# One pool for values and joining gate, running products behind the next subtraction, and an uneven share of filler in a stick-breaking attention block

## The chip, the cores and the metric

The kernel runs on one core of one Trainium2 chip. The time is device microseconds of that core, from one launch; lower is better. The time before is the median of three runs.

## The reference

One decoder block on a sequence of 1024 tokens with 1024 channels and 16 heads of 64, float32 throughout. Two branches start from one normalized input, are gated, and are joined.

```python
def stick_breaking_attention(q, k, v):
    # A[t,s] = sigmoid(z_ts) * prod_{s<j<t} (1 - sigmoid(z_tj)), s < t
    ...
    z = jnp.einsum('bhqd,bhkd->bhqk', qb, kb).astype(jnp.float32) * SB_SCALE
    ...
    w = jnp.where(mask, jnp.exp(jax.nn.log_sigmoid(z) + suffix), 0.0)
    outs.append(jnp.einsum('bhqk,bhkd->bhqd', w.astype(vb.dtype), vb))

def hybrid_layer(x, c, ...):
    mod = jax.nn.silu(c) @ w_ada + b_ada
    shift, scale, gate = jnp.split(mod, 3, axis=-1)
    h = rms_norm(x, norm_gain) * (1.0 + scale[:, None, :]) + shift[:, None, :]
    q, k, v, z_a, u, z_b, m_a, m_b = jnp.split(h @ w_in, offs, axis=-1)
    attn = stick_breaking_attention(to_heads(q), to_heads(k), to_heads(v))
    p_a = (attn * jax.nn.silu(z_a)) @ w_branch_a
    pooled = multiscale_causal_pool(u, pool_w, pool_scale)
    p_b = (pooled * jax.nn.silu(z_b)) @ w_branch_b
    merged = jax.nn.sigmoid(m_a) * p_a + jax.nn.sigmoid(m_b) * p_b
    return x + gate[:, None, :] * (merged @ w_out)
# the output is rms_norm of this
```

## The kernel before

The sequence is held in reverse order, so that the product over the tokens between a key and its query becomes a running product from left to right. Every float32 operand of a large matmul is split in two parts, a high one (a cast by ScalarE, `act.copy`) and a low one (a subtraction, mostly by VectorE), and a product is three matmuls: high x high, high x low, low x high. So wherever a matmul has a new operand, a cast and a subtraction stand before it.

**Order of the work.** A planner places the instructions: it takes the program as traced, simulates it with costs of its own, and on each engine and each queue issues next the earliest traced instruction that is ready in its simulation. An instruction called through `order(...)`, while `pinned` is set, is fixed behind the instruction traced before it on its engine. All matmuls of the attention are pinned, and so are the products `be * om`. The subtractions of the turns, the casts and (before) the scans are not. A buffer's next user waits for the last reader of that buffer. A pool that closes gives its memory to later pools, whose tiles wait for those tiles that had lain in their place.

**Stages, in order of time.** Input norm and modulation; the pooling branch's projection `u`; the values (`seven("v", ...)`, tiles named `vp`); the joining gate m_b (`seven("m", ...)`, tiles `mp`); the gate z_b of the pooling branch (`wzb`); the product with `w_branch_b` (`bp`); the attention with the remaining projections between its parts; the product with `w_branch_a`, the join and the product with `w_out`.

**seven().** A 1024x1024x1024 product as seven products of 512x512x512 instead of eight (p1, p5, p6, p7, p4, p3, p2, in this order), each of 2 x 24 matmuls. Its weights come by SyncE's DMA queue (`raw(first, ...)`): the first operand of a sum into a buffer `raw` of the pool `wts`, which all stages share, the other one (`a22`, `a11s`, `a21d`) into a buffer `ar` of the pool that is handed in as `sums`. Both have two buffers. For p5, `a_s1` loads `a21`, `a22` and `a11s`, adds the first two (L576), and subtracts `a11s` (L578) into `s2k`, which p6 and p3 read again. Then `a_op` makes the cast (L548) and the low part (L549), and `b_op` the same for the other operand (`bhl`, L554, L555). The profile drops digits from names: `ma` is `a11`, `a12`, `a21` or `a22` of the gate, `ma11s` its `a11s`, `va` the values' loads. The values use the pool `vs`, stored through `vo` buffers by `values`. That pool is closed and the pool `ms` is opened for the gate, whose results go through `go` buffers.

**Attention.** Eight pairs of heads; in each pair eight units (p, h, t), a head h and a quarter t of the queries (two rows of 128 queries, widths W from 1024 down to 128), in the order `HT_ORDER`: t = 0, 2, 0, 2, 1, 3, 1, 3. One step of the loop belongs to each unit, so a pair has steps 0 to 7. A step holds:

- `av_items(unit)`: for each chunk of 256 keys (4, 2, 4, 2, 3, 1, 3, 1 chunks in steps 0 to 7) a *turn* and a product. A turn transposes the weights of the chunk two further on (`wt`, into one of two PSUM banks `tr`), casts them (L947), subtracts (L948) and calls `flush()`. At the end `finish` adds the halves of the result (`tp`, L974).
- `z_items` of the unit three further on (t = 2, 1, 3, 1, 3, 0, 2, 0 in steps 0 to 7): logits (`z`), two sigmoids (`om` = 1 - beta, L921, and `be` = beta, L922), a mask by GpSimd (L926), a scan over `om` (the running product, L928) and the product `be * om`. The product is not issued there: it is put on the list `behind` and issued by the next `flush()`.
- a number of *quanta* of the projections (`fill`), three 512 wide matmuls each (`p`). A pair gets 55 of them, shared by `SHARE`:

```python
upto = QUANTA[p] * sum(SHARE[:k + 1]) // sum(SHARE)
step(ahead.get(p * 8 + k, []), p * 8 + k, upto - used)
```

With the even `SHARE` this is 6, 7, 7, 7, 7, 7, 7, 7. Within a step the quanta are spread evenly between the items. The projections' own VectorE work is a subtraction or product per half tile of eight quanta (`klo`, `qlo`, `za`); GpSimd makes the low parts of their weights (`w`, L116).

Lines that the text speaks of: `flush` and `behind`, `z_items` (L902 to 931 of the kernel before), `turn` (L933), `finish` (L964), `step` (L1022).

Of the kernel before, what the change touches and what calls it, by code (L numbers as in the profile page):

```python
# [9 lines left out]
F32 = mybir.dt.float32  # L10
F32R = mybir.dt.float32r
# [4 lines left out]
P = 128  # L16
# [10 lines left out]
NBE = (4, 4)  # L27
SHARE = (7,) * 8
DEPTH = 2
# [22 lines left out]
def block_kernel(ctx, tc, a, out):  # L52
# [3 lines left out]
    def pool(name, **kw):  # L56
        return tc.tile_pool(name=name, bufs=1, reuse_waits="tile", **kw)
# [500 lines left out]
    def k2(t, q):  # L558
        return t[:, 2 * q:2 * q + 2]
# [5 lines left out]
    def seven(nm, sums, load, b_of, a_moves, ta, tb, final, direct):  # L565

        s2k = sums.tile([P, 4, 512], F32, name=nm + "s2k")

# [62 lines left out]

    with pool("vp") as vp:

# [33 lines left out]

        def h_parts(nm, pl):
            def of(name, q):
                if name in ("p1", "p2", "p3"):  # L670
                    k, n = dict(p1=(0, 0), p2=(1, 0), p3=(1, 1))[name]
                    return lambda m, e: hT[:, m, 4 * k + 2 * q + e, 512 * n:512 * n + 512]
                return b_op(k2(tq[("p5", "p6", "p7", "p4").index(name)], q), pl, 2, f"{nm}{name}b{q}")
            return of

        with pool("vs", side="right") as vs:

            def load_v_w(t, m, k, q):
                nc.sync.dma_start(t.rearrange("p k c -> p (k c)"), a["w_v"][m, 2 * k + q])

            def values(m, n, j, src):
                sb = 4 * n + j
                vo = vs.tile([P, 8, 2, HD], F32R, tag="vo", bufs=3, name=f"vo{sb}_{m}")
                pv = src.rearrange("p (h d) -> p h d", d=HD)
                act.copy(vo[:, :, 0], pv)
                v.tensor_sub(vo[:, :, 1], pv, vo[:, :, 0].bitcast(F32))
                nc.sync.dma_start(
                    v_d[4 * m:4 * m + 4, :, sb].rearrange("n p c -> p n c"),
                    vo.rearrange("p (n h) i d -> p n (h i d)", h=2).bitcast(F32),
                )  # L690

            seven("v", vs, load_v_w, h_parts("v", vs), True, ("av", "tr"), ("pj", "z"), values, True)

        with pool("ms", side="right") as ms:

            def load_m_w(t, m, k, q):
                nc.sync.dma_start(t.rearrange("p k c -> p (k c)"), a["w_mb"][m, 2 * k + q])

            def gate_b(m, n, j, src):
                t = ms.tile([P, 512], F32, tag="go", bufs=3, name=f"sb{4 * m + j}_{n}")  # L700
                act.activation(t, src, AF.Sigmoid)
                nc.sync.dma_start(sb_d[4 * m + j][:, 512 * n:512 * n + 512], t)

            seven("m", ms, load_m_w, h_parts("m", ms), False, ("pj", "z"), ("av", "tr"), gate_b, True)

# [68 lines left out]
    with pool("at") as at:  # L774
# [63 lines left out]
        def projections():  # L838
# [16 lines left out]
            for i, (ct, p, use) in enumerate(todo):  # L855
# [6 lines left out]
                if gate:  # L862
                    out_ = sigmoid_out(at, 3, use[p], f"m{ct}")
                for sh in range(2):
# [37 lines left out]
        def z_items(u):  # L902
# [4 lines left out]
            for qb in (2 * t, 2 * t + 1):  # L907
                n0 = qb * P
                W = S - n0
                om = atz.tile([P, S], F32, tag="om", bufs=2, name=f"om{p}_{h}_{qb}")  # L910
                g = t // 2
# [3 lines left out]
                for i in range(nch):  # L915
# [11 lines left out]
                    if i == nch - 1:  # L927
                        v.tensor_tensor_scan(om[:, :W], om[:, :W], om[:, :W], 1.0, ALU.mult, ALU.min)  # L928
                        behind.append(lambda be=be, om=om, W=W: order(v.tensor_mul)(be[:, 1:W], be[:, 1:W], om[:, :W - 1]))
                        rows.append(be)  # L930
# [33 lines left out]
        def finish(u):  # L964
# [4 lines left out]
            if h == 0:  # L969
                both[t] = at.tile([P, 256], F32, tag="tp", bufs=3, name=f"tp{p}_{t}")  # L970
            tp = both[t]
# [236 lines left out]
```

## Time and profile before

| | |
|---|---|
| time, median of 3 runs | 1203.88 us (1203.19 to 1203.93) |
| the profiled execution: its time / its span | 1206.08 us / 1204.3 us |
| TensorE busy | 1174.5 us, 98% of the span |
| VectorE busy | 861.4 us, 72% |
| ScalarE busy | 563.9 us, 47% |
| GpSimd busy | 241.6 us, 20% |
| granted TensorE clock, mean | 0.996 |
| scans `om` (L928) | 128, 183.6 us |
| products `be` | 128, 101.1 us |
| subtractions `wt` (L948) | 160, 99.0 us |

How to read the profile: an engine is busy while an instruction runs on it. Matmuls are pipelined and their ends are modelled, so a busy TensorE isn't necessarily at its peak. A row of the groups has the line, the engine, the operation, output and inputs, shapes and count, then busy time, the mean length of one in ns, the idle time before these instructions and what ended it. A row in order of time has start, length in us, engine and operation, and in brackets the idle time before it and what ended that. A row of a stretch has its bounds and length, and then for each engine its busy time and number of instructions, the granted clock, the busy share of the DMA engines and GB/s.

### The profile page before, as it was taken

Reading aid. Unit: us, or ns where it says so; the run is one execution under the profiler, and the core shown is the slowest. Engines: PE = TensorE matmul, PEld = TensorE weight load, DVE = VectorE, ACT = ScalarE, POOL = GpSimd, SP = SyncE. Lnnn points to the kernel's source line nnn. Section 1 sums busy time; section 2 is a strip of 40 time slices with the busy share of each in tenths; the row PEclk is TensorE's granted clock in tenths of the full one; section 3 lists DMA queues with packets and bytes.
Section 4 is the critical chain, followed back from the end, with each engine's and each line's share of the span. In section 5 each row is a group of like instructions: output and inputs, shape, how many; then the busy total and the mean of one; then the engine's idle time right before and its main releaser. Section 6 shows DMA issues by size and latency. Waiting matters only on the chain.

```text
span 1204.3 us, 15853 instructions
## 1 busy us (share of the span) xinstructions
PE 1174.5 (98%) x5602; PEld 976.4 (81%) x5602; DVE 861.4 (72%) x1135; ACT 563.9 (47%) x1042; POOL 241.6 (20%) x376
## 2 busy tenths in 40 slices
PE   8999999899999999999999999999999999999997
PEld 7888888688888887887788878887878888888886
DVE  5767466554997651887888888879788885785643
ACT  5561363363223432656566566665656654232211
POOL 1000000000000003334343443435344441000001
PEclk9999999899999999999999999999999999999999
DMA  9652339546634357232323132422423115975612
GB/s 346 259 186 100 122 106 309 179 137 241 216 106 158 103 176 219 75 93 85 82 71 113 63 104 72 122 71 88 106 83 88 49 66 197 333 267 168 224 65 79
DMA packets 74753, 172.51 MB, mean 143 GB/s; under 512 B 9393, under 2 KB 22833, under 8 KB 72498
## 3 DMA queue, kind: packets, MB, share of 16 engines
q1 hardware_dynamic: 68770, 160.82, 40.9%
q10 hardware_dynamic: 5904, 10.68, 2.5%
q8 instruction: 44, 0.72, 0.2%
q14 instruction: 35, 0.29, 0.1%
HBM read 121.14 MB, written 33.56 MB: 128 GB/s over the span
## 4 chain that ended last, share of the span: by engine, by line
PE 81%; DVE 7%; issue 4%; DMA 4%; ACT 2%; POOL 1%; SPq 0%; POOLq 0%; ACTq 0%; DVEq 0%
PE p L101 21%; PE wzb L101 7%; PE pa L101 7%; PE bp L101 6%; PE o L101 6%; PE vp L101 6%; PE mp L101 5%; PE u L101 5%; PE z L101 4%; PE av L101 4%; PE wt L101 4%; DVE om L928 3%; PE ua L101 3%; PE wm L101 1%; DVE be L101 1%
## 5 line engine op out<-in xcount | busy, mean ns | idle before, releaser
L101 PE MATMUL p<-hT,w 128*128 128x512 f32 x1536 | 392.6, 392 | 0.0
L101 PEld LDWEIGHTS p<-hT,w 128*128 128x128 f32 x1536 | 283.0, 188 | 58.0 <-DVE klo L101 0.3
L928 DVE TENSOR_TENSOR_SCAN om<-om 128x512 f32<-128x512 f32 (+7 forms) x128 | 183.6, 1435 | 52.6 <-POOL om L926 27.4
L116 POOL TENSOR_TENSOR w<-w_raw,w 128x1024 fp32r<-128x1024 f32 x31 | 80.5, 2596 | 458.7 <-ACT w L121 453.6
L921 ACT ACTIVATE om<-z 128x512 f32<-128x512 f32 (+2 forms) x192 | 94.8, 493 | 130.6 <-PE z L101 99.3
L926 POOL TENSOR_SCALAR_AFFINE_SELECT om<-om 128x128 f32<-128x128 f32 x128 | 78.5, 613 | 182.2 <-ACT om L921 162.3
L948 DVE TENSOR_TENSOR wt<-wt,wt 128x512 fp32r<-128x512 f32 (+1 forms) x160 | 99.0, 620 | 20.8 <-ACT wt L947 20.3
L947 ACT CAST wt<-wt 128x512 fp32r<-128x512 f32 (+1 forms) x160 | 88.1, 551 | 46.8 <-PE wt L101 46.0
L101 PE MATMUL av<-wt,vv 128*128 128x512 f32 x320 | 106.0, 412 | 0.3 <-DVE wt L948 0.3
L101 PE MATMUL wt<-ident,be 128*128 128x128 f32 x576 | 90.8, 274 | 13.0 <-DVE wt L948 8.7
L101 DVE TENSOR_TENSOR be<-be,om 128x511 f32<-128x511 f32 (+7 forms) x128 | 101.1, 794 | 1.1
L922 ACT ACTIVATE be<-z 128x512 f32<-128x512 f32 (+2 forms) x192 | 94.1, 490 | 0.0
L101 PEld LDWEIGHTS wt<-ident,be 128*128 128x128 f32 x576 | 68.8, 140 | 30.1 <-DVE wt L948 9.3
L101 PE MATMUL pa<-ga,wa 128*128 128x512 f32 x384 | 89.6, 389 | 0.1
L101 PE MATMUL o<-wo,mhl 128*128 128x512 f32 (+1 forms) x408 | 89.6, 377 | 0.0
L101 PE MATMUL wzb<-hT,wzb 128*128 128x512 f32 x384 | 87.2, 389 | 0.0
L101 PEld LDWEIGHTS o<-wo,mhl 128*128 128x128 f32 x408 | 73.5, 188 | 14.1
L101 PEld LDWEIGHTS pa<-ga,wa 128*128 128x128 f32 x384 | 72.0, 188 | 15.4 <-DVE wa L116 0.5
L101 PEld LDWEIGHTS wzb<-hT,wzb 128*128 128x128 f32 x384 | 72.1, 188 | 15.0
L101 PE MATMUL z<-kl,q 128*128 128x512 f32 (+2 forms) x192 | 65.5, 341 | 0.0
L101 PE MATMUL z<-kh,q 128*128 128x512 f32 (+2 forms) x192 | 64.1, 334 | 1.3 <-DMA q<-qlo 1.3
L101 PE MATMUL u<-hT,wg 128*128 128x512 f32 x240 | 55.5, 391 | 0.0
(261 smaller groups left out, 1692.4 us busy)
## 6 DMA issues: line engine op xcount, KB each, us to landing
w_raw<-in_w_in SPq DMA_DIRECT2D x32, 512.0 KB, 3.5
v_d<-vo SPq DMA_DIRECT2D x16, 512.0 KB, 4.2
vv<-v_d SPq DMA_DIRECT2D x8, 1024.0 KB, 5.3
wa_raw<-in_w_branch_a SPq DMA_DIRECT2D x16, 512.0 KB, 4.6
wa<-in_w_mod SPq DMA_DIRECT2D x7, 1024.0 KB, 7.0
kh<-kh SPq DMA_DIRECT2D x48, 128.0 KB, 2.3
va<-in_w_v SPq DMA_DIRECT2D x10, 512.0 KB, 3.6
ma<-in_w_mb SPq DMA_DIRECT2D x10, 512.0 KB, 4.5
```

The source lines that it names most:

```text
L101: ins = op(*args, **kw)
L116: lo_eng.tensor_tensor(lo, src, hi.bitcast(F32), op=ALU.subtract)
L921: act.activation(om[:, b0:b0 + n], zp[:, :n], AF.Sigmoid, scale=-0.125)
L922: act.activation(be[:, b0:b0 + n], zp[:, :n], AF.Sigmoid, scale=0.125)
L926: gp.affine_select(out=tl[:, :P], in_=tl[:, :P], pattern=[[1, P]], compare_op=ALU.is_gt, fill=fill, base=0, channel_multiplier=-1)
L928: v.tensor_tensor_scan(om[:, :W], om[:, :W], om[:, :W], 1.0, ALU.mult, ALU.min)
L947: act.copy(wt[:, 0, :off], pt[:, :off])
L948: v.tensor_sub(wt[:, 1, :off], pt[:, :off], wt[:, 0, :off].bitcast(F32))
```

## The change

Four edits:

1. The pools `vs` and `ms` become one pool `vs`, which the values and the gate both use; it stays open until the gate is done, and closes together with the pool `vp`. The tile `s2k` gets one tag for all users, with one buffer.
2. The scan is no longer issued when its row's sigmoids are. It goes on the list `behind` together with its product, both pinned: so `flush()` issues them behind the subtraction of the next turn.
3. `SHARE` becomes 6, 8, 4, 8, 4, 9, 6, 10, which with 55 quanta a pair is also the number of quanta in steps 0 to 7.
4. `om` has three buffers instead of two; `sg` (sigmoid outputs of the other gate) and `tp` have two instead of three.

```diff
-SHARE = (7,) * 8
+SHARE = (6, 8, 4, 8, 4, 9, 6, 10)
...
-        s2k = sums.tile([P, 4, 512], F32, name=nm + "s2k")
+        s2k = sums.tile([P, 4, 512], F32, tag="s2k", bufs=1, name=nm + "s2k")
...
-    with pool("vp") as vp:
+    with ExitStack() as vps:
+
+        vp = vps.enter_context(pool("vp"))
...
+        vs = vps.enter_context(pool("vs", side="right"))
...
-        with pool("vs", side="right") as vs:
...
-            seven("v", vs, load_v_w, h_parts("v", vs), True, ("av", "tr"), ("pj", "z"), values, True)
-
-        with pool("ms", side="right") as ms:
...
-            def gate_b(m, n, j, src):
-                t = ms.tile([P, 512], F32, tag="go", bufs=3, name=f"sb{4 * m + j}_{n}")
...
-            seven("m", ms, load_m_w, h_parts("m", ms), False, ("pj", "z"), ("av", "tr"), gate_b, True)
...
+        def gate_b(m, n, j, src):
+            t = vs.tile([P, 512], F32, tag="go", bufs=3, name=f"sb{4 * m + j}_{n}")
...
+        seven("v", vs, loads("w_v"), h_parts("v"), True, ("av", "tr"), ("pj", "z"), values, True)
+        seven("m", vs, loads("w_mb"), h_parts("m"), False, ("pj", "z"), ("av", "tr"), gate_b, True)
...
-                    out_ = sigmoid_out(at, 3, use[p], f"m{ct}")
+                    out_ = sigmoid_out(at, 2, use[p], f"m{ct}")
...
-                om = atz.tile([P, S], F32, tag="om", bufs=2, name=f"om{p}_{h}_{qb}")
+                om = atz.tile([P, S], F32, tag="om", bufs=3, name=f"om{p}_{h}_{qb}")
...
-                        v.tensor_tensor_scan(om[:, :W], om[:, :W], om[:, :W], 1.0, ALU.mult, ALU.min)
-                        behind.append(lambda be=be, om=om, W=W: order(v.tensor_mul)(be[:, 1:W], be[:, 1:W], om[:, :W - 1]))
+
+                        def weights(be=be, om=om, W=W):
+                            order(v.tensor_tensor_scan)(om[:, :W], om[:, :W], om[:, :W], 1.0, ALU.mult, ALU.min)
+                            order(v.tensor_mul)(be[:, 1:W], be[:, 1:W], om[:, :W - 1])
+
+                        behind.append(weights)
...
-                both[t] = at.tile([P, 256], F32, tag="tp", bufs=3, name=f"tp{p}_{t}")
+                both[t] = at.tile([P, 256], F32, tag="tp", bufs=2, name=f"tp{p}_{t}")
```

More of the change, by code (lines that the diff above doesn't have):

```diff
@@ L666, in block_kernel, with h_parts @@
         early.close()
-        def h_parts(nm, pl):
+        vs = vps.enter_context(pool("vs", side="right"))
+        def h_parts(nm):
             def of(name, q):
@@ L672, in of @@
                     return lambda m, e: hT[:, m, 4 * k + 2 * q + e, 512 * n:512 * n + 512]
-                return b_op(k2(tq[("p5", "p6", "p7", "p4").index(name)], q), pl, 2, f"{nm}{name}b{q}")
+                return b_op(k2(tq[("p5", "p6", "p7", "p4").index(name)], q), vs, 2, f"{nm}{name}b{q}")
             return of
-        with pool("vs", side="right") as vs:
[L678 to L690, printed above, removed]
-            seven("v", vs, load_v_w, h_parts("v", vs), True, ("av", "tr"), ("pj", "z"), values, True)
@@ L694, in block_kernel, with loads, load @@
-        with pool("ms", side="right") as ms:
-            def load_m_w(t, m, k, q):
-                nc.sync.dma_start(t.rearrange("p k c -> p (k c)"), a["w_mb"][m, 2 * k + q])
-            def gate_b(m, n, j, src):
-                t = ms.tile([P, 512], F32, tag="go", bufs=3, name=f"sb{4 * m + j}_{n}")
-                act.activation(t, src, AF.Sigmoid)
-                nc.sync.dma_start(sb_d[4 * m + j][:, 512 * n:512 * n + 512], t)
-            seven("m", ms, load_m_w, h_parts("m", ms), False, ("pj", "z"), ("av", "tr"), gate_b, True)
+        def loads(w):
+            def load(t, m, k, q):
+                nc.sync.dma_start(t.rearrange("p k c -> p (k c)"), a[w][m, 2 * k + q])
+            return load
@@ new lines, in values @@
+        def values(m, n, j, src):
+            sb = 4 * n + j
+            vo = vs.tile([P, 8, 2, HD], F32R, tag="vo", bufs=3, name=f"vo{sb}_{m}")
+            pv = src.rearrange("p (h d) -> p h d", d=HD)
+            act.copy(vo[:, :, 0], pv)
+            v.tensor_sub(vo[:, :, 1], pv, vo[:, :, 0].bitcast(F32))
+            nc.sync.dma_start(
+                v_d[4 * m:4 * m + 4, :, sb].rearrange("n p c -> p n c"),
+                vo.rearrange("p (n h) i d -> p n (h i d)", h=2).bitcast(F32),
+            )
@@ L706, in block_kernel @@
+        def gate_b(m, n, j, src):
+            t = vs.tile([P, 512], F32, tag="go", bufs=3, name=f"sb{4 * m + j}_{n}")
+            act.activation(t, src, AF.Sigmoid)
+            nc.sync.dma_start(sb_d[4 * m + j][:, 512 * n:512 * n + 512], t)
+        seven("v", vs, loads("w_v"), h_parts("v"), True, ("av", "tr"), ("pj", "z"), values, True)
+        seven("m", vs, loads("w_mb"), h_parts("m"), False, ("pj", "z"), ("av", "tr"), gate_b, True)
     turns[0] = cycle(("av", "tr", "pj", "z"))
```

## The prediction

> **What bounds the kernel now.** I read the page first: busy times, then the forty slices.
>
> ```profile
> span 1204.3 us, 15853 instructions
> PE 1174.5 (98%) x5602; PEld 976.4 (81%) x5602; DVE 861.4 (72%) x1135; ACT 563.9 (47%) x1042; POOL 241.6 (20%) x376
> PE   8999999899999999999999999999999999999997
> DVE  5767466554997651887888888879788885785643
> PEclk9999999899999999999999999999999999999999
> ```
>
> TensorE is the bound: 1174.5 of 1204.3 us busy. None of its matmuls is removed, so the change can only take back idle time, 29.8 us in all, and time lost to a low clock. Two places stand out: the eighth slice, the only one with a lower granted clock, and the attention (slices 17 to 34), where VectorE is at 8 tenths.
>
> I then asked for stretches around the eighth slice and, for that place, the instructions in order of time.
>
> ```profile
> 215.00:240.00 25.00, 20.30 (x76) 15.88 (x75) 16.29 (x14) 8.22 (x10) 0.00 (x0) 0.86 0.44 151
> 240.00:265.00 25.00, 25.00 (x112) 20.70 (x111) 13.25 (x14) 16.16 (x22) 0.00 (x0) 1.00 0.38 124
> 220.00:225.00 5.00, 5.00 (x12) 3.94 (x13) 2.51 (x4) 1.04 (x1) 0.00 (x0) 0.50 0.90 313
> ...
> 147.95 1.23 DVE L583 TENSOR_TENSOR va11d<-va11d,va21d 128x1024 f32<-128x1024 f32 x1 [0.22 <-DMA va11d<-in_w_v]
> 205.01 11.04 PE L101 MATMUL mp<-hT,mp1a 128*128 128x512 f32 x48
> 209.55 1.28 SPq L697 DMA_DIRECT2D ma<-in_w_mb  x1
> 217.64 1.23 DVE L576 TENSOR_TENSOR ma<-ma,ma 128x1024 f32<-128x1024 f32 x1 [0.52 <-DMA ma<-in_w_mb]
> 218.90 1.04 ACT L548 CAST mp5a<-ma 128x1024 fp32r<-128x1024 f32 x1 [1.76 <-DVE ma L576]
> 220.00 13.95 PE L101 MATMUL mp<-mp5b,mp5a 128*128 128x512 f32 x48 [3.95 <-ACT mp5a L548]
> ```
>
> The columns after the length are PE, weight load, VectorE, ScalarE, GpSimd, granted clock, DMA share, GB/s. This is the gate's second product, p5. Its weight load `a22` is issued only at 209.55, the add that needs it starts at 217.64, the cast at 218.90, and TensorE stands still for 3.95 us. Then the clock is granted at 0.50 for the next 5 us (12 matmuls, no idle time shown). The stretch holds 76 matmuls where the next equal one holds 112: 36 matmuls at 25/112 = 0.223 us, so 8.0 us are lost here, idle and low clock together.
>
> For the attention I cut the time at the first matmul of each pair of heads (found by counting matmuls in program order) and asked what TensorE's transposes waited for.
>
> ```profile
> 502.30:566.28 63.98, 63.02 (x326) 52.96 (x325) 53.80 (x73) 40.19 (x87) 25.85 (x38) 1.00 0.27 77
> 566.28:632.72 66.44, 63.27 (x326) 52.82 (x325) 56.61 (x76) 39.96 (x86) 26.60 (x41) 1.00 0.32 87
> 891.89:957.79 65.90, 63.32 (x327) 52.87 (x325) 56.81 (x75) 39.73 (x86) 26.91 (x39) 1.00 0.30 85
> ...
> 549.62:558.99 9.37, 8.41 (x42) 6.61 (x41) 9.37 (x13) 4.05 (x9) 2.08 (x4) 1.00 0.01 2
> 617.41:625.43 8.02, 8.02 (x42) 6.69 (x41) 7.66 (x11) 5.09 (x10) 4.53 (x4) 1.00 0.00 1
> ...
> PE wt L101 <- DVE wt L948: 8.7, 9, 1.8
> PE wt L101 <- POOL tp L977: 2.2, 3, 1.1
> PE wt L101 <- DVE be L101: 1.9, 4, 0.6
> ```
>
> A pair without any wait: pair 0 took 63.98 us and had waits in one step alone, step 6, 9.37 us where the same step of pair 1 took 8.02; so 62.6 us. The first seven pairs run from 502.30 to 957.79, 455.5 us; seven quiet ones are 438.2. The prize here is 17.3 us. All of it is transposes waiting for VectorE: for the subtraction that frees their PSUM bank (both first rows; GpSimd is only named as the last releaser), or for a row of weights that isn't multiplied yet (`be`). VectorE is busy 53.8 to 56.8 us of a pair, so it has room on average and is late only in places:
>
> ```profile
> 686.52 1.67 DVE L101 TENSOR_TENSOR be<-be,om 128x895 f32<-128x895 f32 x2
> 687.74 0.30 PE L101 MATMUL wt<-ident,be 128*128 128x128 f32 x1 [0.59 <-DVE be L101]
> 697.61 2.40 POOL L116 TENSOR_TENSOR w<-w_raw,w 128x1024 fp32r<-128x1024 f32 x1 [1.75 <-ACT w L121]
> 697.69 0.60 PE L101 MATMUL wt<-ident,be 128*128 128x128 f32 x4
> 698.38 0.59 ACT L947 CAST wt<-wt 128x512 fp32r<-128x512 f32 x1
> 698.51 3.38 DVE L928 TENSOR_TENSOR_SCAN om<-om 128x896 f32<-128x896 f32 x1
> 702.37 0.69 DVE L948 TENSOR_TENSOR wt<-wt,wt 128x512 fp32r<-128x512 f32 x1
> 703.21 0.52 PE L101 MATMUL wt<-ident,be 128*128 128x128 f32 x3 [1.12 <-POOL tp L977]
> ```
>
> At 703.21 TensorE waits for the subtraction at 702.37, which stood behind a scan of 3.38 us; at 687.74 it waits for the product at 686.52.
>
> **The change, part by part.**
>
> *One pool.* The gate's `a22` and `a11s` loads go into the two `ar` buffers. In one pool these are free once the values' last reader of them is done, 147.95 + 1.23, instead of when the old pool's memory comes free; the two loads can be issued some 60 us earlier and also leave the crowded stretch around 210. Then the other operand, `a21`, waits only for the shared `raw` buffer as before, and the chain add 1.23, cast 1.04 starts when p1 is still running (until 216.05): it has to be 4 us earlier, and its late part is gone. I take 7.5 of the 8.0 us. Bounds: all 8.0; and 2.7, if `a21` or the second half now comes last and half the idle time and a third of the clock loss are saved (3.95/2 + 2.3/3; 2.3 is 22.4 - 12 matmuls at 0.223). The pool is larger by what only one side used (`vo` or `go`), so the later pools may wait for other buffers: the next stretches have no idle TensorE (240 to 265 above), and I cost that at nothing; if the cover failed it would be one wait for a load, up to 4 us like this one. `s2k` shared: its reader in the values ends with p3, before the gate's p5 writes it; nothing.
>
> *Scan behind the next subtraction.* No instruction is added or removed. The durations are those of the attention's groups (the last row is the page's, for GpSimd):
>
> ```profile
> L948 DVE TENSOR_TENSOR wt<-wt,wt 128x512 fp32r<-128x512 f32 x96 | 64.6, 673 | 11.4 <-ACT wt L947 11.1
> L974 DVE TENSOR_TENSOR tp<-av,tp 64x256 f32<-64x256 f32 x128 | 52.7, 413 | 2.6
> L928 DVE TENSOR_TENSOR_SCAN om<-om 128x896 f32<-128x896 f32 x15 | 33.5, 2231 | 0.4 <-ACT om L921 0.3
> L928 DVE TENSOR_TENSOR_SCAN om<-om 128x1024 f32<-128x1024 f32 x14 | 32.6, 2328 | 21.3 <-POOL om L926 12.0 <-ACT om L921 9.3
> L928 DVE TENSOR_TENSOR_SCAN om<-om 128x768 f32<-128x768 f32 x16 | 28.9, 1804 | 6.5 <-POOL be L926 3.4 <-ACT om L921 1.9 <-POOL om L926 1.1
> L928 DVE TENSOR_TENSOR_SCAN om<-om 128x640 f32<-128x640 f32 x16 | 27.7, 1730 | 5.1 <-ACT om L921 4.8 <-POOL be L926 0.3
> L928 DVE TENSOR_TENSOR_SCAN om<-om 128x512 f32<-128x512 f32 x15 | 18.5, 1235 | 1.7 <-POOL om L926 1.7
> L101 DVE TENSOR_TENSOR be<-be,om 128x1023 f32<-128x1023 f32 x14 | 18.1, 1291 | 0.0
> L101 DVE TENSOR_TENSOR be<-be,om 128x895 f32<-128x895 f32 x15 | 17.6, 1174 | 0.0
> L116 POOL TENSOR_TENSOR w<-w_raw,w 128x1024 fp32r<-128x1024 f32 x31 | 80.5, 2596 | 458.7 <-ACT w L121 453.6
> ```
>
> Before, a scan may start as soon as its sigmoids are there, so up to 2.3 us stand ahead of a subtraction. After, the subtraction goes first, and scan and product, 3.6 us for the longest row, stand behind it. The price: the rows get their weights later, and VectorE may idle where a scan is ready and its subtraction isn't. The tightest place is the row of 896 of the next pair, made at the end of step 5. Its scan now waits for step 6's first subtraction: transposes and cast (as from 697.69 to 698.97 above, 1.3 us), the subtraction 0.67, scan 2.23, product 1.17, together 5.4 us after the step begins, if VectorE is then free; wanted by the third turn of step 6, two thirds of 7.3 us plus its logits, about 5.2. So about 0.2 us of wait where VectorE is on time.
>
> *Shares.* A quantum is three matmuls, 0.67 us by the 0.223 above. VectorE's own work in a step is the scans and products of the two rows it makes, one subtraction a turn and two 0.41 us adds. Step 5 and step 7 (rows of 1024 and 896): 2.33 + 2.23 + 1.29 + 1.17 + 0.67 + 0.83 = 8.5 us. Steps 1 and 3 (768, 640; two turns): 1.80 + 1.73, about 0.95 + 0.8 for the products by their length, 1.3 + 0.83: 7.4. Steps 0 and 6 (512, 384), by length: about 7 and 6.3; steps 2 and 4 (256, 128): about 5.3 and 4.7. TensorE without waits, before: 8.3, 7.7, 8.7, 7.7, 7.6, 7.3, 8.0, 7.3 (sum 62.6). So steps 5 and 7 are over by 1.2 us each, which lands in the steps after them, 6 and 0: there lie the waits above (549.62 is a step 6, 697.69 a step 0). The quanta were 6 and then 7 a step; with 6, 8, 4, 8, 4, 9, 6, 10 TensorE's steps become 8.3, 8.4, 6.7, 8.4, 5.6, 8.6, 7.3, 9.3, each at or above VectorE's work.
>
> Following one pair through in these numbers leaves waits where turns come fastest: about 0.7 us in step 2 (its first subtraction behind scan and product of 640 and two adds), 0.3 in step 4, 0.2 in step 6; 1.2 us a pair against 17.3/7 = 2.5. That gives 7 x 1.3 = 9 us. The projections' six subtractions a pair (0.68 us each) and the scan blocked by GpSimd will fall badly in some pairs; I take 7. Bounds: all 17.3; and a loss of 5, if each pair's step 6 waits for the whole scan and product of 896 (3.4 us, less the 2.5 that go: 0.9 x 7 = 6, less a little at the others).
>
> *The rest, costed at nothing.* A third `om` buffer covers the rows' later release. `sg` and `tp` go from three buffers to two: the next user of a slot comes at least a whole step (5.6 us) after the store was issued. If that cover were gone, ScalarE would stand still for a store's landing. The query projection finishes four quanta closer to the step that uses it (7 quanta where 11 in the sixth pair, about 8.6 us, for a cast, a subtraction and one move); SP's queue order is otherwise unchanged.
>
> *A rule against the row at 698.51.* That scan of 896 took 3.38 us where its kind takes 2.23 on average; it began inside the 2.40 us GpSimd subtraction and ended 1.88 us after that one's end, so it looks as if it stood still until then: 1.15 us lost. The Trainium skill, "SBUF — State Buffer", section "Who interferes with whom", says that a VectorE instruction with two SBUF inputs and a GpSimd instruction that reads SBUF exclude each other, the later one waiting for the whole of the first; by that rule scan and product, now back to back, are one stretch of 3.4 us to be hit, and the 7 us of the attention would shrink towards nothing. This row agrees with it. From the rows alone: there are 31 such GpSimd subtractions in the kernel, some four a pair; two more hits a pair at 1.15 us would be 16 us of VectorE time, as much as the waits I expect to go. That is in rival (1).
>
> **Sum.** 7.5 + 7 = 14.5. The profiled execution took 1206.08 us (span 1204.3), the median of the runs 1203.88; I count from the median: 1189.4 us.
>
> **The rivals.**
> (1) The pool works, the shares and the scan order give nothing: late weights, and two more GpSimd hits a pair, replace the waits removed. For it: VectorE needs 54 to 57 us of a 62.6 us pair whatever the order. Against: the waits sit where the step sums say. 1203.9 - 7.5, within 3: 1196.
> (2) The pool doesn't do what it says: the load is issued early but the other half comes last. For it: the DMA share is 0.90 in the stretch from 220. Then 2.7 + 7: 1194.
> (3) Slower: the 896 row decides. If VectorE enters step 6 over 3.5 us late in every pair (a collision of 2.4 plus two projection subtractions), the third turn waits 4 us, 28 us in seven pairs against 17.3 + 7.5 saved: 1207. It decides from 3.9 us a pair on.
> (4) Both work fully, 1203.9 - 8 - 15: 1181.
>
> **How the numbers follow.** A time that differs by less than 0.2% (2.4 us) can't be told from no change here. Forecast 0.6 (its own range 1184 to 1194), (1) 0.18, (2) 0.07, (3) 0.05, (4) 0.06, a remainder of 0.04 for no net change. The range 1183 to 1199 leaves out (3), (4) and the remainder. Faster 0.91 (the forecast, (1), (2), (4)), same 0.04, slower 0.05.
>
> **What would show it.** Right: no lower clock in the eighth slice, `a22` of the gate issued before 200, about 112 matmuls in each 25 us there; pairs of 63 to 65 us; transposes waiting less for the subtraction, more for `be`. Wrong: a step 6 over 9 us in most pairs, or TensorE idle where the gate or the pooling gate begins.

## The result and the profile after

The changed kernel takes 1222.03 us (median of 4 runs, 1218.52 to 1225.31), the kernel before 1203.91 us on the same chip: 1.0149 times as long (95% interval 1.0115 to 1.0182). The forecast was 1189.4 us, the range 1183 to 1199: the change is slower, on the other side. The profiled execution is the longest of the four, 1225.31 us.

The page of the changed kernel, busy times and slices:

```profile
span 1223.6 us, 15848 instructions
PE 1177.8 (96%) x5602; PEld 978.5 (80%) x5602; DVE 866.7 (71%) x1135; ACT 566.1 (46%) x1042; POOL 253.1 (21%) x376
PE   8999999999999999999999989999999899999997
DVE  5767567456987623968898787878788875785642
PEclk9999999999999999999999999999999999999999
```

The low clock of the eighth slice is gone, and TensorE has the same 5602 matmuls, but it is now idle for 45.8 us (1223.6 - 1177.8) instead of 29.8. In the attention two of its slices, the 24th and the 32nd, fall below 9 tenths.

Stretches of the changed kernel: the two around the gate's p5; two pairs of heads, cut as in the prediction (first and seventh); and four neighbouring steps of the sixth and seventh pair (5, 6, 7 and the next 0).

```profile
215.00:240.00 25.00, 24.39 (x108) 19.85 (x107) 12.45 (x11) 11.28 (x15) 0.00 (x0) 1.00 0.38 136
240.00:265.00 25.00, 25.00 (x112) 20.72 (x111) 14.29 (x14) 13.60 (x20) 0.00 (x0) 1.00 0.51 167
...
498.38:564.24 65.86, 63.19 (x327) 53.00 (x325) 52.08 (x72) 40.80 (x87) 30.15 (x38) 1.00 0.28 80
902.57:971.65 69.08, 63.65 (x326) 52.93 (x325) 55.90 (x74) 39.97 (x86) 27.95 (x39) 1.00 0.28 80
...
876.03:884.68 8.65, 8.65 (x42) 7.24 (x41) 4.19 (x6) 6.30 (x12) 3.47 (x5) 1.00 0.40 105
884.68:893.23 8.55, 7.56 (x39) 6.11 (x38) 8.45 (x12) 4.26 (x9) 2.63 (x4) 1.00 0.00 1
893.23:902.57 9.34, 9.34 (x45) 7.75 (x44) 6.12 (x8) 6.42 (x12) 4.14 (x6) 1.00 0.32 104
902.57:912.42 9.85, 8.58 (x46) 7.00 (x45) 9.62 (x13) 4.95 (x10) 3.54 (x5) 1.00 0.52 156
```

The gate behaves as forecast: 108 matmuls where there were 76, 24.39 of 25 us busy. The attention does not. In the step 5 from 876.03 TensorE never waits and VectorE is busy 4.19 of 8.65 us; in the step 6 behind it VectorE is busy 8.45 of 8.55 us and TensorE stands still for 1 us. The same again in steps 7 and 0: 6.12 of 9.34, then 9.62 of 9.85. VectorE's work was meant to be evened out, and it comes in blocks.

The two profiled spans differ by 19.3 us. The first pair begins at 498.38 instead of 502.30 (3.9 us won), the attention from there to its last product takes 537.0 instead of 513.9 us (23.1 lost), and what follows takes 0.1 us more. The 3.9 is what is left of some 8 us won at the gate, for this reason, in order of time (SyncE's queue, TensorE, VectorE, TensorE):

```profile
145.72 0.33 SPq L682 DMA_DIRECT2D ma<-in_w_mb  x1
148.82 0.33 SPq L682 DMA_DIRECT2D ma11s<-in_w_mb  x1
...
228.14 2.14 PE L101 MATMUL mp<-mp6b,mp6a 128*128 128x512 f32 x8 [0.61 <-DVE mp6b L555]
...
459.53 0.69 DVE L101 TENSOR_TENSOR klo<-p,kh 128x512 fp32r<-128x512 f32 x1 [12.87 <-DMA pb_d<-bs]
460.28 16.17 PE L101 MATMUL p<-hT,w 128*128 128x512 f32 x63 [3.42 <-DVE klo L101]
```

These two loads of the gate go out at 145.72 and 148.82 instead of from 209.55 on, and 0.61 us of waiting is left. But at 459.53 the first low part of the keys (`klo`) waits for a store of the pooling branch, and TensorE for it, 3.42 us. The clock is then granted at 0.57 on average from 461 to 465, with 13 matmuls in these 4 us where a full clock gives 18. The profile names the store; that the tile now lies where the store's source lay is a reading of it.

Where the attention loses, by TensorE's waits (us in total, times, longest) from 498.3 to 1036 us in the changed kernel:

```profile
PE wt L101 <- DVE wt L950: 14.5, 12, 2.5
PE wt L101 <- DVE be L101: 11.3, 8, 2.5
PE wt L101 <- POOL tp L979: 3.6, 7, 1.4
```

Each of the three rows that stood in the prediction (8.7, 1.9 and 2.2) has grown; the wait for `be`, a row whose weights aren't made yet, is six times what it was.

### The profile page after: what moved, and what is told of

Same layout as the page of the kernel before. It is cut to its first block, busy times and chain, and to the rows that moved or that the text cites. A ratio compares the mean times of both kernels' runs of the same rounds, so it can differ in the third digit from the quotient of the medians.

```text
span 1223.6 us, 15848 instructions
## 1 busy us (share of the span) xinstructions
PE 1177.8 (96%) x5602; PEld 978.5 (80%) x5602; DVE 866.7 (71%) x1135; ACT 566.1 (46%) x1042; POOL 253.1 (21%) x376
## 4 chain that ended last, share of the span: by engine, by line
PE 75%; DVE 8%; issue 8%; POOL 4%; DMA 3%; ACT 2%; SPq 0%; POOLq 0%; DVEq 0%; ACTq 0%
PE p L101 19%; PE wzb L101 7%; PE pa L101 7%; PE o L101 6%; PE bp L101 6%; PE vp L101 6%; PE u L101 4%; PE mp L101 4%; PE z L101 4%; PE wt L101 3%; PE av L101 3%; PE ua L101 3%; DVE om L101 2%; DVE be L101 2%; POOL om L924 1%
## 5 line engine op out<-in xcount | busy, mean ns | idle before, releaser
L101 DVE TENSOR_TENSOR_SCAN om<-om 128x512 f32<-128x512 f32 (+7 forms) x128 | 176.7, 1381 | 2.0 <-POOL om L924 2.0
L924 POOL TENSOR_SCALAR_AFFINE_SELECT om<-om 128x128 f32<-128x128 f32 x128 | 87.7, 685 | 204.8 <-ACT om L919 178.8
L101 PE MATMUL wt<-ident,be 128*128 128x128 f32 x576 | 92.4, 276 | 30.3 <-DVE wt L950 14.5
L101 DVE TENSOR_TENSOR be<-be,om 128x511 f32<-128x511 f32 (+7 forms) x128 | 114.4, 894 | 5.1
L101 PEld LDWEIGHTS wt<-ident,be 128*128 128x128 f32 x576 | 69.4, 141 | 49.0 <-DVE be L101 13.1
```

Of the source, the lines that this page charges most:

```text
L101: ins = op(*args, **kw)
L924: gp.affine_select(out=tl[:, :P], in_=tl[:, :P], pattern=[[1, P]], compare_op=ALU.is_gt, fill=fill, base=0, channel_multiplier=-1)
```

## The experiments

All times are medians, ratios are to the kernel before on the same chip, with 95% intervals. "Late" is the changed kernel's order (scan and product behind the next subtraction). A step deals its items, the turns and the logits, into groups, and each group is followed by its part of the quanta. "Not past a group" is the late order, but in a group without a turn the block of scan and product is issued at the group's end. Kernels with a late or pinned scan have the changed buffers, the others those of before.

| run | pool | scan | shares | GpSimd's low part | us | ratio |
|---|---|---|---|---|---|---|
| pool_only | one | at once | even | whole | 1198.4 | 0.9945 (0.9926 to 0.9964) |
| pool_buffers | one, changed buffers | at once | even | whole | 1198.3 | 0.9942 (0.9924 to 0.9960) |
| pool_share | one | at once | changed | whole | 1207.3 | 1.0009 (0.9997 to 1.0022) |
| pool_scan | one | late | even | whole | 1222.2 | 1.0130 (1.0107 to 1.0152) |
| scan_pinned_at_once | one | at once, pinned | even | whole | 1201.3 | 0.9958 (0.9942 to 0.9974) |
| scan_flush_each_group | one | late, but not past a group | even | whole | 1195.9 | 0.9914 (0.9888 to 0.9939) |
| scan_behind_memset | one | late | even | zeros | 1199.0 | 0.9936 (0.9913 to 0.9959) |
| pool_memset | one | at once | even | zeros | 1185.9 | 0.9830 (0.9807 to 0.9854) |
| pool_memset_long | one | at once | even | zeros, three times | 1187.2 | 0.9845 (0.9829 to 0.9861) |
| groups_new_shares | one | not past a group | changed | whole | 1207.1 | 1.0006 (0.9992 to 1.0020) |
| groups_mild_shares | one | not past a group | mild | whole | 1194.2 | 0.9903 (0.9887 to 0.9919) |
| groups_low_in_four | one | not past a group | even | four pieces | 1193.5 | 0.9899 (0.9877 to 0.9920) |
| share_memset | one | at once | changed | zeros | 1184.5 | 0.9829 (0.9812 to 0.9845) |
| changed_memset | one | late | changed | zeros | 1201.3 | 0.9967 (0.9956 to 0.9979) |
| groups_mild_four | one | not past a group | mild | four pieces | 1189.8 | 0.9874 (0.9859 to 0.9889) |
| pool_mild_four | one | at once | mild | four pieces | 1191.4 | 0.9886 (0.9871 to 0.9900) |

**One part at a time.** From the changed kernel, taken back:

```diff
# pool_only: all three.  pool_buffers: the first two.  pool_share: the last two.  pool_scan: the first
-SHARE = (6, 8, 4, 8, 4, 9, 6, 10)
+SHARE = (7,) * 8
...
-                        def weights(be=be, om=om, W=W):
...
-                        behind.append(weights)
+                        v.tensor_tensor_scan(om[:, :W], om[:, :W], om[:, :W], 1.0, ALU.mult, ALU.min)
+                        behind.append(lambda be=be, om=om, W=W: order(v.tensor_mul)(be[:, 1:W], be[:, 1:W], om[:, :W - 1]))
...
-  om bufs=3, sg 2, tp bufs=2
+  om bufs=2, sg 3, tp bufs=3
```

> The kernel before with the one pool alone. The changed kernel's trace shows no 3.95 us wait and no low clock at the gate's p5 any more, so every theory expects 1203.9 - 7 = about 1197 us, unless a merged pool also moves what the attention's first tiles wait for (the wait of 3.4 us before the first low part of k at 460 us in the changed kernel): then about 1200.

> One pool and the uneven shares; scans and buffers as before. Theory late scans (the scan pinned behind the next subtraction leaves VectorE idle in steps 5 and 7 and then stands between two subtractions in steps 6 and 0): the shares alone help or do nothing, 1188 to 1197 us, waits in steps 6 and 0 under 1 us. Theory fast turns (with 4 quanta in steps 2 and 4 the turns follow each other too fast for VectorE): the shares lose by themselves, 1203 us or more, with waits in steps 2 and 4.

> One pool, the scan behind the next subtraction, the changed buffers, and the even shares. Late scans: 1212 to 1222 us, with waits in steps 6 and 0 as in the changed kernel. Fast turns: 1197 to 1203 us, because no step has fewer than six quanta.

> One pool and the buffer counts alone (three om, two sg, two tp); even shares and free scans. If the 3.4 us wait at the attention's start comes from where the tiles now lie, it shows here: about 1197 + 3.5 = 1200 us, with the first low part of k waiting for a store of the pooling branch. If it comes from the order of the instructions: 1197 us. ScalarE's waits for a free om buffer (15 us in the kernel before) should be gone in both.

The pool wins 7.5 us (1198.4 from 1205.9), which is the 7.5 of the prediction. The buffers change the sum by nothing, but they bring the wait for the store. The first low part of the keys in pool_only, then in pool_buffers:

```profile
451.22 0.69 DVE L101 TENSOR_TENSOR klo<-p,kh 128x512 fp32r<-128x512 f32 x1 [5.87 <-ACT kh L814]
```

```profile
456.32 0.69 DVE L101 TENSOR_TENSOR klo<-p,kh 128x512 fp32r<-128x512 f32 x1 [10.74 <-DMA pb_d<-bs]
```

TensorE waits 1.28 us for it in pool_buffers and not at all in pool_only. Of the two answers expected for pool_buffers neither is whole: the wait comes with the buffers, but it is shorter there than the 3.42 us of the changed kernel, and the time isn't 1200.

The scan's move costs 23.9 us (1222.2 against 1198.3), and the shares 8.9 us (1207.3 against 1198.4), so both parts that were forecast as a gain are losses, each by itself. Together they cost no more than the scan alone (1222.0). The largest of TensorE's waits from 470 to 1036 us, in pool_scan, then pool_share, then pool_only:

```profile
PE wt L101 <- DVE be L101: 14.4, 7, 2.9
PE wt L101 <- DVE wt L950: 11.4, 12, 3.2
```

```profile
PE wt L101 <- DVE wt L946: 14.2, 17, 1.9
```

```profile
PE wt L101 <- DVE wt L946: 8.0, 8, 1.8
PE wt L101 <- POOL tp L975: 5.2, 4, 3.0
```

They fail in two ways. The late scan makes waits for `be`, seven of them, two us each, about one a pair. The shares make twice as many waits for the subtraction (17 instead of 8). The profiled execution of pool_share took 1211.8 us, more than its median; its attention alone is 8.7 us longer than that of pool_only (524.8 against 516.1).

**Why the late scan loses: pinned, or late?** There are two theories: pinning the scan takes a freedom from the planner that it needs, or the next subtraction comes too late. One run pins the scan where it was, the other keeps it behind the next subtraction, unless the group of items has no turn: then it is issued at the group's end.

```diff
# scan_pinned_at_once, from pool_scan
-                        def weights(be=be, om=om, W=W):
...
+                        order(v.tensor_tensor_scan)(om[:, :W], om[:, :W], om[:, :W], 1.0, ALU.mult, ALU.min)
# scan_flush_each_group, from pool_scan, in step()
                 for g in group:
                     next(g)
+                if i >= 0 and main not in group:
+                    flush()
```

> As pool_scan (one pool, changed buffers, even shares), but the scan is pinned where it is traced, right after its row's sigmoids; only the product waits for the next subtraction, as in the kernel before. Late scans: the 24 us that pool_scan lost over pool_only come back, 1196 to 1201 us, waits in step 6 below 1 us a pair. If it is the pinning itself that costs (VectorE's order no longer free for the planner): 1210 us or more.

> As pool_scan, but the list of scans and products is also emptied in each group of a step that has no turn, so scan and product stand behind a subtraction only where a turn stands in the same group (steps 5 and 7 have one turn, in the third of four groups). Late scans: the waits in step 6 (19.8 us over eight pairs in pool_scan) fall to 5 us or less and those in step 0 to 8 to 11; 1198 to 1206 us. If the block of scan and product between two subtractions is the cost, wherever it stands: 1212 us or more.

Pinning costs about 2.9 us (1201.3 against 1198.4; the intervals overlap). With the block issued in groups without a turn the 24 us are gone (1195.9, 26 less than pool_scan), and no wait for `be` is left; the first row of its waits:

```profile
PE wt L101 <- DVE wt L950: 11.5, 13, 1.6
```

So it is the lateness, and the groups without a turn make it. Steps 5 and 7 have one turn each, in the third of four groups, and they make the longest rows, 1024 and 896. The block of 1024, ready after the second group, waits for that one subtraction; the block of 896 waits for the next step's first. What VectorE waited for in the attention of the changed kernel says so (scans, subtractions: busy, mean ns, idle before):

```profile
L101 DVE TENSOR_TENSOR_SCAN om<-om 128x640 f32<-128x640 f32 (+3 forms) x123 | 167.8, 1364 | 2.0 <-POOL om L924 2.0
L950 DVE TENSOR_TENSOR wt<-wt,wt 128x512 fp32r<-128x512 f32 (+1 forms) x159 | 99.3, 626 | 78.4 <-ACT wt L949 77.9
```

and the same groups of the kernel before:

```profile
L928 DVE TENSOR_TENSOR_SCAN om<-om 128x640 f32<-128x640 f32 (+3 forms) x123 | 174.8, 1422 | 47.8 <-POOL om L926 27.0 <-ACT om L921 16.2 <-POOL be L926 3.6
L948 DVE TENSOR_TENSOR wt<-wt,wt 128x512 fp32r<-128x512 f32 (+1 forms) x159 | 98.4, 620 | 20.8 <-ACT wt L947 20.3
```

Before, VectorE's idle time stood ahead of scans: it waited for rows. Now almost none stands there (2.0), and 78.4 us stand ahead of subtractions, behind which the scans are fixed. The trace tells how much of it a scan could have used, if a row is called ready when its last sigmoid and its mask have ended: VectorE is idle while a ready scan hasn't started for 53.8 us in the changed kernel, 37.7 of them with a row of 1024, and for 4.5 us in the kernel before; in scan_flush_each_group it is 16.4, of which rows of 1024 have 2.2. The time isn't used, and the block runs when TensorE needs its result.

**What GpSimd has to do with it.** Rival theories for the rest: reads by GpSimd, which hold up scans and products; or GpSimd's time as such, or VectorE's order alone. In these kernels GpSimd writes zeros instead of the low part of the projections' weights, so that the product of low x high adds nothing; in the long one it does so three times over, which takes it longer than the subtraction.

```diff
# in split(); pool_memset from pool_only, scan_behind_memset from pool_scan
         copy_to(hi_eng, hi, src)
+        if lo_eng is gp:
+            gp.memset(lo.bitcast(F32), 0.0)        # pool_memset_long: three times
+            return hi, lo
         lo_eng.tensor_tensor(lo, src, hi.bitcast(F32), op=ALU.subtract)
```

> As pool_only, with the same zeros instead of GpSimd's subtraction. What the collisions cost with the free scans: four scans lie stretched in the kernel before, whose waits make about 4 us of TensorE time, so 1193 to 1196 us against 1198.4. If collisions are nothing: 1198.

> As pool_scan, but GpSimd writes zeros to the low parts of the projections' weights in the attention instead of subtracting: the low x high product adds nothing, and GpSimd no longer reads two inputs for 2.4 us some four times a pair. Theory collisions (scans and products held up by that GpSimd subtraction make the 24 us): 1205 us or less. Late scans: collisions are a part only, 1210 to 1218 us, and step 6 still waits at least 1 us in every pair.

> As pool_memset (zeros instead of the low parts of the projections' weights), but GpSimd writes the zeros three times, about 2.9 us in all, longer than the subtraction of 2.4 to 2.6 us that it replaces. If it is GpSimd's reading that holds up VectorE (scan and product read two inputs from SBUF): no change against pool_memset, 1186 to 1188 us. If it is GpSimd's time (masks queue behind the weights' low part, and scans wait for masks): 1195 us or more, near pool_only's 1198.

GpSimd's groups for the low part from 502 to 1000 us in pool_only, then pool_memset_long:

```profile
L116 POOL TENSOR_TENSOR w<-w_raw,w 128x1024 fp32r<-128x1024 f32 x26 | 66.7, 2564 | 59.4 <-ACT w L121 59.4
```

```profile
L118 POOL MEMSET w<- 128x1024 f32 x78 | 74.4, 954 | 34.1 <-PE p L101 31.9
```

26 subtractions of 2.56 us are 12.5 us dearer (1198.4 against 1185.9) than writes, and 78 writes, 74.4 us of them, are no dearer than 26 (1187.2, intervals overlap). So it isn't GpSimd's time. Writes also don't wait for ScalarE's cast, as the subtractions do (59.4 us in the first row above), so masks might come sooner behind them; but VectorE is idle ahead of scans for the masks of `om` as long in pool_memset as in pool_only (26.5 and 27.0 us). That leaves the reading, and it cost more than twice the 2.4 to 5.4 us that I had expected.

The traces show it case by case. In pool_only, from the attention on, nine scans and products start while a GpSimd subtraction is running, and each ends after that subtraction's end by its own shortest length less about 0.1 us, as if it had stood still until then. (A tenth starts while GpSimd's subtraction, 3.44 us long, is itself held up.) In pool_memset_long 28 start while GpSimd writes, and none is over 0.1 us longer than the shortest of its kind. The turns' subtractions, which have one of their two inputs in PSUM, aren't held up by reads either: 23 start inside one in pool_only, and none is over 0.3 us longer than the shortest of its kind.

With the late scan the reads cost 23.2 us (1222.2 against 1199.0), and the late scan without them still costs 13.0 (1199.0 against 1185.9). Its 24 us are thus about 13 of lateness and about 11 of more, or more harmful, collisions; neither theory alone has it. There are more: scans and products that last over 0.8 us longer than the shortest of their kind and length are 13 in pool_scan and 7 in pool_only, in one profile each. The waits in scan_behind_memset, and the first row of pool_memset:

```profile
PE wt L101 <- DVE be L101: 9.6, 7, 1.7
PE wt L101 <- DVE wt L953: 6.0, 7, 2.0
```

```profile
PE wt L101 <- DVE wt L949: 5.5, 7, 1.0
```

**Why the shares lose.** My theory then was that four quanta in steps 2 and 4 let the turns come faster than VectorE can subtract, whatever else goes on; the rival was that the shares are right and collisions fall where no room is left. A milder set, the changed set with timely scans, and both with writes only:

```diff
# groups_new_shares, groups_mild_shares: from scan_flush_each_group.  share_memset, changed_memset:
# pool_share and the whole changed kernel, with the memset above
-SHARE = (7,) * 8
+SHARE = (6, 8, 4, 8, 4, 9, 6, 10)
+SHARE = (7, 7, 6, 7, 6, 7, 7, 8)
```

> As scan_flush_each_group, with the changed kernel's uneven shares. If the shares lose by themselves, as pool_share against pool_only says (9 us): 1202 to 1208 us, waits in steps 4 and 2 (4 quanta) up. If they lost only because scans were in the planner's places for the even shares: 1190 to 1196 us.

> As scan_flush_each_group, with shares 7, 7, 6, 7, 6, 7, 7, 8: one quantum less in steps 2 and 4, one more in steps 0 and 7, where the waits of step 0 begin. Fast turns: steps 2 and 4 stay quiet at 6 quanta and step 0's 10 us of waits fall by some 3 to 5: 1190 to 1194 us. If the shares don't matter at this size: 1195 to 1197 us.

> As pool_share (one pool, uneven shares, free scans), with GpSimd writing zeros to the low parts of the projections' weights instead of subtracting. To be held against pool_memset, 1185.9 us. Fast turns: steps 2 and 4 still wait, 1190 us or more. Collisions only: the 9 us that the shares lost are gone, 1185 to 1188 us.

> The changed kernel as a whole, with the same zeros. Held against scan_behind_memset, 1199.0 us, it tells what the uneven shares are worth to late scans without collisions. Fast turns: 1202 us or more. If shares fitted to VectorE's work help as the change means them to: 1190 to 1196 us.

The changed shares cost 11.2 us also with timely scans (1207.1 against 1195.9). But without GpSimd's reads they lose nothing (1184.5 against 1185.9, intervals overlap), and the largest kind of wait in share_memset is this:

```profile
PE wt L101 <- DVE wt L949: 1.6, 4, 0.6
```

So my theory fell: with scans issued at once, turns aren't too fast for VectorE, and the shares lose only where GpSimd reads. The count of scans and products that lasted over 0.8 us longer than the shortest of their kind is 7 in pool_only, 11 in pool_share, and none in the kernels with writes only. TensorE's excess is each start's distance to the one before, less the usual distance of the same two kinds of instruction. In pool_share seven of the 11 lie in odd steps, each with 1.5 to 3.6 us of excess in the step behind it, 14.5 us together; in pool_only two do, with 2.1 and 0.9 us. That the shares take from steps 2 and 4 the room that absorbed a collision is a reading of this: more collisions fall into the odd steps too, and no run separates the two. The excess by step, summed over the eight pairs, shows the shift:

| excess in us | step 0 | step 2 | step 4 | step 6 |
|---|---|---|---|---|
| before | 10.9 | 2.9 | 1.7 | 4.4 |
| pool_only | 13.0 | 2.8 | 1.6 | 4.3 |
| pool_share | 6.4 | 4.9 | 9.6 | 7.3 |
| pool_memset | 7.5 | 0.8 | 0.4 | 1.4 |
| share_memset | 2.6 | -0.2 | 1.7 | 1.2 |
| pool_scan | 15.1 | 4.2 | 1.1 | 19.8 |
| changed | 13.1 | 5.2 | 6.4 | 14.3 |
| groups_mild_four | 7.2 | 1.8 | 0.6 | 2.0 |

The shares take from step 0, as meant, and with GpSimd reading they pay in steps 2, 4 and 6; without, the sum of these steps falls from 10.1 to 5.3, of which the times show 1.5 us (intervals overlap). With late scans even the writing kernel gains nothing from them (1201.3 against 1199.0). The mild set is within the noise of even shares (1194.2 against 1195.9, intervals overlap).

**Shorter collisions, and a better version.** If reads block for a whole instruction, shorter ones block for less:

```diff
# in split(); groups_low_in_four from scan_flush_each_group; groups_mild_four with the mild shares as well;
# pool_mild_four: four pieces and mild shares on pool_only
         copy_to(hi_eng, hi, src)
+        if lo_eng is gp:
+            for k in range(0, shape[1], 2):
+                gp.tensor_tensor(lo[:, k:k + 2], src[:, k:k + 2], hi[:, k:k + 2].bitcast(F32), op=ALU.subtract)
+            return hi, lo
```

> As scan_flush_each_group, with GpSimd's subtraction for the weights' low part cut in four of a quarter the width. If GpSimd and VectorE shut each other out for a whole instruction, the longest hold is about 0.7 us instead of 2.4: 1188 to 1193 us, and no scan stretched by more than a microsecond. If the two share the port evenly, the pieces change nothing: 1195 to 1198 us.

> Everything that helped, nothing left out: one pool, scan and product issued at once where the group has no turn, shares 7, 7, 6, 7, 6, 7, 7, 8, GpSimd's subtraction in four pieces. The gains of the shares (1.8) and of the pieces (2.5) add up: 1191 to 1192 us. If both only remove the same waits: 1193 to 1194.

> One pool, the free scans and the buffers of the kernel before, the mild shares, and GpSimd's subtraction in four pieces. Collisions: the pieces give 3 to 5 us against pool_only's 1198.4 and the shares 1 to 3: 1191 to 1195 us. If the gains belonged to the flush in each group: 1196 to 1198.

Four pieces give 2.5 us (1193.5 against 1195.9; the intervals overlap), and no scan or product is stretched by over 0.8 us any more, although GpSimd is busy longer with them. The collisions are shorter, not gone: all scans and products together last 13.5 us longer than the shortest of their kinds, where it is 25.5 us in scan_flush_each_group and 5 to 6 with writes only.

```profile
L118 POOL TENSOR_TENSOR w<-w_raw,w 128x256 fp32r<-128x256 f32 x106 | 89.8, 877 | 58.0 <-ACT w L125 58.0
```

All that helped together, with nothing left out of the computation, takes 1189.8 us: 1.26% less than the kernel before (1.11 to 1.41%). On the same chip the version without the scan's move takes 1191.4, so the move in its mended form gives 1.6 us, which can't be told from nothing (intervals overlap).

## Why the prediction was wrong

**One pool: right.** 7.5 us were forecast and 7.5 measured, by the steps foreseen: early issue, no 0.50 clock, and in pool_only 112 matmuls from 215 to 240. That the two figures are the same is luck; the interval goes from 4.3 to 8.9 us. The later pools' places, costed at nothing, cost nothing in pool_only. The wait of the changed kernel at 460.28, which looks like their "one wait for a load, up to 4 us", comes with the buffers of "The rest, costed at nothing". That paragraph looked at when the slots of `om`, `sg` and `tp` are used again, and not at other tiles that would have to wait; pool_buffers shows that it cost nothing in sum there.

**The scan: the step-6 sum failed.** The prediction set 5.4 us (transposes and cast 1.3, subtraction 0.67, scan 2.23, product 1.17) against 5.2 wanted: "about 0.2 us of wait where VectorE is on time". That last condition was never priced. The rows of the sixth pair, steps 5 and 6, of the changed kernel in order of time:

```profile
879.13 0.61 ACT L919 ACTIVATE om<-z 128x512 f32<-128x512 f32 x1
881.92 0.69 DVE L950 TENSOR_TENSOR wt<-wt,wt 128x512 fp32r<-128x512 f32 x1 [2.89 <-ACT wt L949]
882.52 2.28 DVE L101 TENSOR_TENSOR_SCAN om<-om 128x1024 f32<-128x1024 f32 x1
885.04 1.21 DVE L101 TENSOR_TENSOR be<-be,om 128x1023 f32<-128x1023 f32 x1
885.37 0.59 ACT L919 ACTIVATE om<-z 128x512 f32<-128x512 f32 x1
886.33 0.61 ACT L949 CAST wt<-wt 128x512 fp32r<-128x512 f32 x1
887.10 0.67 DVE L950 TENSOR_TENSOR wt<-wt,wt 128x512 fp32r<-128x512 f32 x1
887.70 2.00 DVE L101 TENSOR_TENSOR_SCAN om<-om 128x896 f32<-128x896 f32 x1
889.63 0.52 DVE L950 TENSOR_TENSOR wt<-wt,wt 128x384 fp32r<-128x384 f32 x1
890.08 1.07 DVE L101 TENSOR_TENSOR be<-be,om 128x895 f32<-128x895 f32 x1
891.21 0.33 PE L101 MATMUL wt<-ident,be 128*128 128x128 f32 x1 [0.99 <-DVE be L101]
```

Step 6 begins at 884.68. Its first subtraction starts 2.42 us later, not 1.3. The 1.3 was read at 697.69, where a step 0 begins with its transposes; step 6 begins with two logits, 0.46 us, and its cast stood behind a sigmoid of a projection and two of the row that step 6 makes on ScalarE. Another subtraction slipped in between scan and product (the two are pinned, it isn't). The product ends at 891.15, 6.5 us after the step's start; TensorE wanted it at about 890.2. No collision is in it, and the wait lasts 1 us. In the earlier step VectorE idled 2.89 us ahead of the one subtraction at 881.92, with the row of 1024 behind it, whose last sigmoid for the scan had ended at 879.74. Where a collision comes on top, as in the third pair, it is worse. GpSimd's row, VectorE's and TensorE's, and then the same kernel's stretches:

```profile
676.05 0.69 DVE L950 TENSOR_TENSOR wt<-wt,wt 128x512 fp32r<-128x512 f32 x1 [5.17 <-ACT wt L949]
678.25 2.88 POOL L116 TENSOR_TENSOR w<-w_raw,w 128x1024 fp32r<-128x1024 f32 x1 [2.35 <-ACT w L121]
679.18 3.04 DVE L101 TENSOR_TENSOR be<-be,om 128x1023 f32<-128x1023 f32 x1
686.58 0.48 PE L101 MATMUL wt<-ident,be 128*128 128x128 f32 x1 [2.22 <-DVE be L101]
```

```profile
685.00:686.00 1.00, 0.00 (x0) 0.00 (x0) 1.00 (x3) 0.05 (x1) 0.41 (x2) 1.00 0.00 0
687.00:688.00 1.00, 1.00 (x4) 0.81 (x3) 0.90 (x2) 0.54 (x2) 0.00 (x0) 0.50 0.08 16
690.00:691.00 1.00, 1.00 (x6) 0.82 (x5) 0.97 (x3) 0.15 (x1) 0.00 (x0) 1.00 0.00 0
```

VectorE idles 5.17 us; its product then starts inside GpSimd's subtraction and takes 3.04 us where 1.21 is usual, ending 1.09 after that one's end. Everything behind it is late, the row of 896 is missed by 2.22 us, and the clock is then at half for another 3 us, so that a us holds 4 matmuls instead of 6.

**Rivals.** (3), a chance of 0.05, had the place ("the 896 row decides") and the sign; its price was 28 us in seven pairs and only from 3.9 us of lateness on, with collisions as the cause. Measured: an excess of 19.8 us in step 6 in pool_scan, and still 11.4 in scan_behind_memset, where no scan or product is stretched: lateness that the pairs have by construction, so no mishap was needed. Rival (1), 0.18, had late weights and two more GpSimd hits a pair, and priced them at no more than the waits removed, 1196 us; it had the causes, but not the size. Steps 5 and 7 with a single turn stood in the description of the kernel; the prediction used the number of turns for VectorE's load ("one subtraction a turn") and not for how long `behind` has to wait.

**The reads.** The prediction's sum took 7 us instead of 9 for the projections' subtractions and for scans blocked by GpSimd together; more collisions stood in the rivals (1) and (3) only. They were a term of both edits, about 11 us of the scan's loss and all of the shares': 78 writes cost nothing that could be told where 26 reads cost 12.5 us. The Trainium skill, "SBUF — State Buffer", section "Who interferes with whom", says that reads by GpSimd exclude VectorE instructions with two SBUF inputs and that plain writes don't. Trace and runs agree with that section.

**The shares: the table of steps was sound, its margin wasn't.** With writes only, and scans at once, the set loses nothing, so VectorE's work by step was counted well enough. The 7 us of gain in the attention, of which the shares were to bring a part, became a loss of 8.9 us for the shares alone. The three rows of waits that the prediction showed for its prize also add up to 12.8 us and not to 17.3. The set left steps 2 and 4 with 1.4 and 0.9 us above VectorE's work (6.7 against 5.3, 5.6 against 4.7) where the even shares left 3.4 and 2.9, and the stretched scans and products of pool_share are 1.0 to 2.2 us longer than their kind. By these figures, evening out a margin takes it from where it was used; that this, and not the larger number of collisions in the odd steps, makes the whole loss isn't shown.

## What to carry to other kernels

Work that is put "behind the next X" runs as late as the rarest X allows: before such a move, list for each stage how many X there are and where, and check the one with a single X against the time at which the result is wanted. Idle time ahead of an instruction whose successors on the same engine are ready is the sign of it in a profile. And where two engines collide, shorten or remove the collision first, and share slack out evenly only afterwards, since slack that looks spare in the mean may be what hides the collisions.

## What the runs showed of the hardware

A product or scan on VectorE (two inputs in SBUF) that starts while a GpSimd subtraction of 2.4 us or more is running stands until that one is done: 3.04 us instead of 1.21 in the changed kernel, 4.25 instead of 2.00 in pool_only. There is no such case in pool_memset_long, where GpSimd only writes. With reads in pieces the hold lasts until the piece ends: in groups_low_in_four a scan of 640 that starts inside a piece of 0.73 us takes 1.98 us instead of 1.48.

A wait of TensorE of 2.22 us was followed by a clock of 0.50 over the next 3 us. In pool_scan 1.81 us of waiting before 458.36 were followed by it too, from 459.7 on, while 2.97 us in pool_only left the clock at 1.00: in these traces the length of a wait alone doesn't decide. The Trainium skill, "TensorE: Matmul & The Clock Gate", section "Part 1: The HAM clock gate (the "warmup" mystery)", gives the idle window that leads to half the clock as about 3.4 us. Here shorter waits did it, and the measurement decides.
